# Order of small steps at three joins of a one-core encoder layer on Trainium2: weight parts of the down product, operands of the second branch, a weight cast, and the early weight parts

## The chip, the cores and the metric

The kernel runs on one core of one Trainium2 chip. The metric is the device time of one execution in microseconds (us). The kernel before has a median of 1955.72 us over 3 runs (1953.15 to 1956.71).

The engines are named as the profile names them: PE is TensorE (matmul), PEld its weight load, DVE is VectorE, ACT is ScalarE, POOL is GpSimd, SP is SyncE. SP and POOL issue most of the DMAs; each engine works through its own queue in order.

## The reference, cut to what matters

One layer, for a prompt of 1024 frames and a sample of 32 frames (1056 columns in the kernel, kept as four groups of 264), model width 1024, all in float32:

```python
h = rms_norm(x);  z = h @ w_in                       # q, k, v, gates ...
ya = sink_attention(...);  yb = hgrn2(...)
mix = sigmoid(ga) * (ya @ w_br_a) + sigmoid(gb) * (yb @ w_br_b)
x = x + rms_norm(mix @ w_out, g_post_mix)
a, u = split(rms_norm(x) @ w_up, 2)                  # D_FF = 2816 each
a = conv3(a) + b_conv
x = x + rms_norm((gelu(a) * u) @ w_down, g_post_ffn)
x = x + (pe @ w_ple) * sigmoid(x @ w_ple_gate)
```

The change touches three places of it: the two branch products (`w_br_a`, `w_br_b`) with the mix, the product with `w_out`, and the passage from the last piece of `w_up` to the product with `w_down`.

## The kernel before, in words

**Precision.** Every float32 operand is split into a high and a low part (fp32r). A product is three matmuls: high by high, high by low, low by high. So each weight tile needs, ahead of its product, a load, an ACT cast (the high part) and a DVE subtraction (the low part). In the input and output projections this is `load_next` (L177: ACT L184 and DVE L186). In a variant of it, chosen by `lo_by`, the low part is made by ACT (L188, the negated weight) and a POOL DMA that adds the weight to it (L189). In the branch products it is L228 (ACT) and L229 (DVE). In the up product it is L2029 and L2030, in the down product L2136 and L2137.

**Fewer products.** The branch, up and down products use a seven-product scheme for 2 by 2 blocks: of each unit, seven weight combinations ("parts", index i from 0 to 6) meet seven operand combinations, and DVE and ACT combine the seven results. A part of the branch product is 24 matmuls of 264 columns (two column pieces p, four k slices, three products each).

**Stages around the change.**

- *Branch stage* (849 to about 1020 us of the span). The operands of branch 0 are in tiles `oa`, those of branch 1 in tiles `ob`. For branch 1, `a_load` (L1554) loads an `ob` tile from memory on SP's queue, `b_rest` (L1558) loads more on POOL's, and `a_split` casts it (ACT L1561) and subtracts (DVE L1562, 128 x 1056). `during(s, f, ...)` puts a step into the program behind product number s of the stage; `beside` runs it there. The weights of this stage come in tiles `wa` (SP, L1530). ACT also copies results out of the PSUM banks here (`as`, L1671), and DVE combines them (L1689, L1691, L1693).
- *Out projection* (from 1019.8 us). Its first two weights, called w0 and w1 here, are loaded (`raw_next`) and cast (`load_next` with `lo_by` "dma") while the last branch products run. Blocks of 24 matmuls follow (L205 to L207); between them stand the transposes of `p` (L1980, results copied by DVE L229 into `pc`), the squares of the norm (L1830) and the **early parts**: `early_parts` makes the first seven parts of the up weight and the two halves of `w_ple` in three buffers (`pw`, `place`) and stores each to memory (`pw_d`, POOL, L2066, L2073, L2075). A buffer is written again only when its store has landed. One `next(early)` stands behind each of the nine blocks of `E_AT`.
- *Up units* (to about 1615 us), 22 of them with seven products each. `prepare(n)` makes the part that is AHEAD (3) products later. In the last unit the operands of the down product (`dop`) are loaded and split, too.
- *Down product*. `d_raw` loads two raw parts into one `wd` tile (two buffers, so the fourth load waits until the second tile has been read by L2136 and L2137). `d_prepare(n)` casts parts up to number n and loads two tiles ahead. Its first products go to fresh PSUM banks (three of them), and `evacuate` copies them out by ACT (L2513) to `S_`, `T1_` and the accumulators `acc`. The page that holds `S_` is the one that DVE reads last in the up unit (`Sp`: L2402, L2406, L2409).

**What sets the order.** The kernel is written with a tile framework whose scheduler may move instructions of an engine ahead of one another where no dependency forbids it. `with behind(S, V):` pins the instructions of its block behind what ACT (`S`) and DVE (`V`) were given so far; `behind()` without an engine pins nothing. So both the place in the program and the pin decide where an instruction stands in its engine's queue.

Of the kernel before, what the change touches and what calls it, by code (L numbers as in the profile page):

```python
# [10 lines left out]
F32 = mybir.dt.float32  # L11
# [6 lines left out]
P = 128  # L18
# [3 lines left out]
NF = 22  # L22
# [3 lines left out]
T = 1056  # L26
# [4 lines left out]
H = 264  # L31
# [28 lines left out]
def layer_kernel(  # L60
# [1523 lines left out]
    with right("mp") as mp:  # L1584
# [132 lines left out]
        def during(s, f, *a):  # L1717
            steps_a.setdefault(s, []).append((f, a))
# [14 lines left out]
        for n, (i, p) in enumerate(((2, 1), (3, 0), (3, 1))):  # L1733
            during(2 * n + 1, both, a_split, i, p)
        for n, (i, p) in enumerate((i, p) for i in range(3) for p in range(2)):
            during(18 + 2 * n, a_page, i, p, 1)
            during(18 + 2 * n, a_load, i, p, dma, 1)
            during(19 + 2 * n, b_rest, i, p)
            during(23 + 2 * n, both, a_split, i, p, 1)
        for n, (i, p) in enumerate((i, p) for i in (3, 4, 5) for p in range(2)):  # L1740
            during(34 + n + n // 2, a_page, i, p, 1)
            during(34 + n + n // 2, a_load, i, p, dma, 1)
            during(35 + n + n // 2, b_rest, i, p)
            during(38 + n + n // 2, both, a_split, i, p, 1)
        for p in range(2):
            during(44 + p, a_page, 6, p, 1)
            during(44 + p, a_load, 6, p, dma, 1)
# [5 lines left out]
        for n in range(2):  # L1753
            during(32 + n, mix_load)
            during(54 + 2 * n, raw_next)
            during(57 + 2 * n, both, load_next)
        n_s = [0]

        def beside(n):
# [332 lines left out]

    def prepare(n):

        if n >= 7 * NF:
            d_prepare(n - 7 * NF)
        while n_parts[0] < min(n + 1, 7 * NF):
            u, i = divmod(n_parts[0], 7)
            if i == 0:
                if u not in raw_w:  # L2100
                    unit_raw(u)
                s1 = wp.tile([P, 4, P], F32, tag="wb", name=nm("sa"), bufs=8)[:]
                gens[u] = unit_parts(u, s1, part_tile, lambda i, t: ready_w.append(t))
# [40 lines left out]
    for p in range(2):  # L2144
        for c in range(8):
            if p == 0 and c == 1:
                lo_by[0] = "vector"
            if p and c == 5:
                load_ple()
            with behind(*((S, V) if (p, c) == (0, 1) else ())):  # L2150
                w = next_w(2 + (p and c > 3) - (p + c == 0))
            for g in (2 * p, 2 * p + 1):
                z_out(c, g, block(w, ALL, Ra[g], Rb[g], KO if g % 2 else KS, H))
                if p == 0 and 2 * c + g in E_AT:
                    with behind(*((S, V) if c == 0 else ())):
# [199 lines left out]
    def up_unit(u):  # L2355
# [62 lines left out]
                 (3, Y, False, (3, 8)), (4, Z, False, (4, 6)), (5, Y, False, (2, 5)))  # L2418
        for ps, steps in (((0,), first_), ((1,), early)) if u == 0 else (((0, 1), order),):
            for n, (i, t, first, then) in enumerate(steps):  # L2420
                if u:
                    prepare(7 * u + n + AHEAD)
                elif ps == (1,):
                    with behind(S, V):
                        prepare(n + AHEAD + 2)
                mults(i, t, first, ps)
                if u == NF - 1:
                    if n == 0:
                        d_raw()
                        d_raw()  # L2430
                    if i < 3:
                        for p in range(2):
                            load_op(0, p, i, gdma)
                    if n in (3, 5, 6):
                        split_ops(0, {3: 0, 5: 1, 6: 2}[n])
                if ps == (1,) and n == 1:
                    with behind(E):
                        x1_t.append(pair_norm(1, 1.0 / D, late=True))
                if ps == (1,) and n == 4:
                    with behind(E):  # L2440
                        x1_t[0]()
                for a in then:
                    with behind(*((V,) if ps == (0,) and a == 2 else ())):
                        after(a, ps)
                if n == 1:
                    with behind(V):
                        tail_rest(u)
                if u == 1 and n == 3:
                    with behind(V):
                        tail_rest(0)  # L2450
                if u > 1 and n == 2 + u % 2:
                    if u % 2 == 0:
                        sums_of.append(act_sums(u // 2 - 1))
# [9 lines left out]
    for u in range(NF):  # L2463
        if u == 1:
# [5 lines left out]

    ep = ctx.enter_context(right("ep"))
    nrm = ep.tile([P, 4, 8], F32, name="nrm")
    T1_ = ep.tile([P, 4, 2, H], F32, tag="T1", name="T1")
    acc_t = [ep.tile([P, 4, 2, H], F32, name=f"acc{i}") for i in range(3)]
    last_sums = act_sums(NF // 2 - 1, acc_t[0][:].rearrange("p a b c -> p (a b c)")[:, 0:T + 2],
                         gdma)
    acc_t = [acc_t[1], acc_t[2], acc_t[0]]
    S_ = page(lq, 3, [P, 4, 2, H], "S").bitcast(F32)

    def acc_of(c):  # L2480
# [62 lines left out]
    def d_unit(pt, ph, c, ps=(0, 1), ws=None, beside=None):  # L2543
# [4 lines left out]
        kept = []  # L2548
        for n, i in enumerate(OPS[ph]):
            if ws is None:  # L2550
                d_prepare(n_d[0] + D_AHEAD)
                w = ready_d[n_d[0]]
                n_d[0] += 1
            else:
                w = ws[n]
            kept.append(w)
            t, first = banks[i]
            d_mults(w, pt, i, t, first, ps)
            evacuate(pt, c, i, t, ps)
# [385 lines left out]
```

## Time and profile before

| | |
|---|---|
| median of 3 runs | 1955.72 us |
| profiled execution, time | 1960.47 us |
| its span | 1958.8 us, mean granted PE clock 0.995 |
| PE busy | 1925.3 us (98%) |
| DVE, ACT, POOL busy | 1476.1, 1029.2, 378.9 us |
| DMA, mean | 168 GB/s |

How to read it: times in the trace count from the span's start. In a row of the timeline, the bracket behind an instruction gives the idle time of its engine ahead of it, and what ended that. In a row of the windows stand the stretch, its length, the busy time of PE, PEld, DVE, ACT and POOL with the number of instructions, the granted PE clock, the DMA engines' share and GB/s. In a row of the waits stand an engine, operation and line, what ended its waits, their sum, their number and the longest. In the chain of waits the time is what each piece contributed, which can be less than the instruction's duration.

### The profile page before, as it was taken

What the parts mean: (1) busy time and instruction counts of PE and PEld (TensorE: products, weight loads), DVE (VectorE), ACT (ScalarE), POOL (GpSimd) and SP (SyncE); (2) the same over time, 40 slices, a digit from 0 to 9 for tenths busy, and PEclk for the clock granted to TensorE, in tenths of its full rate; (3) what the DMA queues carried; (4) which work ended last, traced back from release to release, by engine and by line L of the source; (5) the groups of instructions that cost most, each with busy time, mean ns of one, the idle gap of its engine ahead of it and who ended that gap; (6) DMA issues with size and microseconds to landing.
All of it is one profiled execution on the core that took longest, in us unless ns stands there. A gap on an engine that the chain in (4) does not pass through costs nothing.

```text
span 1958.8 us, 38169 instructions
## 1 busy us (share of the span) xinstructions
PE 1925.3 (98%) x14523; PEld 1906.3 (97%) x14523; DVE 1476.1 (75%) x3201; ACT 1029.2 (53%) x2214; POOL 378.9 (19%) x530
## 2 busy tenths in 40 slices
PE   8999999999999999999999999999999998999999
PEld 8999999999999999999999999999999998999998
DVE  6777777788888888666785778788787876668872
ACT  7667777666656666553435763333333336534432
POOL 2111211001101001123221113444645330000000
PEclk9999999999999999999998999999999999999999
DMA  8544543455547354599978584566897456655443
GB/s 266 151 113 122 135 124 98 136 114 138 144 115 181 108 123 87 160 300 286 284 217 278 185 280 128 162 174 189 152 195 172 125 190 195 211 181 159 120 133 89
DMA packets 319599, 329.11 MB, mean 168 GB/s; under 512 B 17432, under 2 KB 277435, under 8 KB 319416
## 3 DMA queue, kind: packets, MB, share of 16 engines
q1 hardware_dynamic: 274152, 218.92, 36.2%
q0 software_dynamic: 45136, 107.70, 23.1%
q8 instruction: 114, 1.87, 0.4%
q14 instruction: 69, 0.57, 0.1%
q10 hardware_dynamic: 128, 0.06, 0.0%
HBM read 234.48 MB, written 132.47 MB: 187 GB/s over the span
## 4 chain that ended last, share of the span: by engine, by line
PE 83%; DVE 5%; DMA 4%; issue 4%; ACT 3%; POOL 0%; SPq 0%; ACTq 0%; DVEq 0%; POOLq 0%
PE st L2374 7%; PE st L2373 7%; PE st L2372 7%; PE st L2498 4%; PE mm L205 4%; PE st L2500 4%; PE mm L207 4%; PE st L2499 4%; PE mm L206 4%; PE st L205 2%; PE st L206 2%; PE st L207 2%; PE Y L1122 2%; PE Y L1125 2%; PE Y L1124 2%
## 5 line engine op out<-in xcount | busy, mean ns | idle before, releaser
L2372 PE MATMUL st<-op,wt 128*128 128x264 f32 x1232 | 348.7, 283 | 1.6 <-DMA wt<-pw_d 0.5
L2374 PE MATMUL st<-op,wt 128*128 128x264 f32 x1232 | 349.8, 284 | 0.0
L2373 PE MATMUL st<-op,wt 128*128 128x264 f32 x1232 | 347.7, 282 | 0.0
L2372 PEld LDWEIGHTS st<-op,wt 128*128 128x128 f32 x1232 | 231.2, 188 | 3.2 <-ACT Sp L2384 0.9
L2373 PEld LDWEIGHTS st<-op,wt 128*128 128x128 f32 x1232 | 231.4, 188 | 0.0
L2374 PEld LDWEIGHTS st<-op,wt 128*128 128x128 f32 x1232 | 230.8, 187 | 0.0
L2498 PE MATMUL st<-dop,wt 128*128 128x264 f32 x616 | 175.4, 285 | 6.3 <-ACT S L2513 6.3
L2500 PE MATMUL st<-dop,wt 128*128 128x264 f32 x616 | 175.3, 285 | 0.0
L2499 PE MATMUL st<-dop,wt 128*128 128x264 f32 x616 | 174.9, 284 | 0.0
L2029 ACT CAST wt<-wu 128x512 fp32r<-128x512 f32 x126 | 76.1, 618 | 177.3 <-POOL wu L2038 69.9
L205 PE MATMUL mm<-La,wh 128*128 128x384 f32 (+1 forms) x480 | 158.2, 330 | 0.0
L206 PE MATMUL mm<-Lb,wh 128*128 128x384 f32 (+1 forms) x480 | 155.3, 324 | 0.6 <-DVE Lb L784 0.4
L207 PE MATMUL mm<-La,wl 128*128 128x384 f32 (+1 forms) x480 | 154.9, 323 | 0.1
L2498 PEld LDWEIGHTS st<-dop,wt 128*128 128x128 f32 x616 | 116.7, 190 | 6.8 <-ACT S L2513 6.7
L2030 DVE TENSOR_TENSOR wt<-wu,wt 128x512 fp32r<-128x512 f32 x126 | 86.4, 694 | 43.0 <-ACT wt L2029 43.0
L2499 PEld LDWEIGHTS st<-dop,wt 128*128 128x128 f32 x616 | 116.7, 189 | 0.0
L2500 PEld LDWEIGHTS st<-dop,wt 128*128 128x128 f32 x616 | 116.4, 189 | 0.0
L2136 ACT CAST wt<-wd 128x512 fp32r<-128x512 f32 (+1 forms) x84 | 49.0, 586 | 96.3 <-PE st L2500 73.5
L206 PEld LDWEIGHTS mm<-Lb,wh 128*128 128x128 f32 x480 | 90.4, 189 | 1.7 <-DVE Lb L784 1.4
L207 PEld LDWEIGHTS mm<-La,wl 128*128 128x128 f32 x480 | 90.2, 188 | 0.5 <-DVE wl L759 0.5
L1122 PE MATMUL G<-La,wt 128*128 128x288 f32 x288 | 90.4, 314 | 0.0
L205 PEld LDWEIGHTS mm<-La,wh 128*128 128x128 f32 x480 | 90.2, 188 | 0.2
(628 smaller groups left out, 6334.1 us busy)
## 6 DMA issues: line engine op xcount, KB each, us to landing
wu<-in_w_up_dram SPq DMA_DIRECT2D x42, 512.0 KB
wu<-in_w_in_dram SPq DMA_DIRECT2D x36, 512.0 KB
w_d<-in_w_down_dram POOLq DMA_DIRECT2D x24, 704.0 KB, 8.7
a_d<-Up SPq DMA_DIRECT2D x21, 528.0 KB
wr<-in_w_in_dram SPq DMA_DIRECT2D x21, 512.0 KB
s_d<-sm SPq DMA_DIRECT2D x40, 264.0 KB
dop<-s_d SPq DMA_DIRECT2D x16, 528.0 KB
wr<-in_w_out_dram SPq DMA_DIRECT2D x16, 512.0 KB
```

Source lines behind the costliest of these rows:

```text
L205: E.matmul(ps, wh, a, start=first and n == 0, stop=False)
L206: E.matmul(ps, wh, b, start=False, stop=False)
L207: E.matmul(ps, wl, a, start=False, stop=last and n == len(ks) - 1)
L1122: E.matmul(o, wh, x[0][k], start=first and k == 0, stop=False, skip_group_check=True)
L2029: S.copy(t[:, 0], src)
L2030: V.tensor_tensor(t[:, 1], src, t[:, 0].bitcast(F32), op=ALU.subtract)
L2372: E.matmul(o, wh, xh, start=first and k == 0, stop=False, skip_group_check=True)
L2373: E.matmul(o, wh, xl, start=False, stop=False, skip_group_check=True)
L2374: E.matmul(o, wl, xh, start=False, stop=k == 3, skip_group_check=True)
L2498: E.matmul(o, wh, xh_, start=first and k == 0, stop=False, skip_group_check=True)
L2499: E.matmul(o, wh, xl_, start=False, stop=False, skip_group_check=True)
L2500: E.matmul(o, wl, xh_, start=False, stop=k == ng - 1, skip_group_check=True)
```

## The change

Four edits; nothing that is computed changes.

1. *Branch stage*. The steps of the second branch's operands get other numbers: loads of the first six at 20 + 2n - n//5 (before 18 + 2n), their splits at 28 + n (before 23 + 2n); the next six loads 2 later, their splits at 41, 42, 44, 45, 46, 47 (before 38, 39, 41, 42, 44, 45).
2. *Second out weight*. The step that casts w1 stands at 58, before at 59.
3. *Early parts*. Each `next(early)` is pinned behind ACT and DVE; before, only the first (c = 0) was.
4. *Last up unit and start of the down product*. The two first `d_raw` stand ahead of the unit's first `prepare`; from the unit's second product on, one down part is made for each product, six in all (before: one for each of its last three, inside `prepare`, when the number passed the end of the up parts, and three more ahead of the first down product). The down parts made at the first two units of the down product are pinned behind ACT and DVE. `T1_` and the three accumulators change places in memory with each other.

```diff
@@ branch stage
-            during(18 + 2 * n, a_page, i, p, 1)
-            during(18 + 2 * n, a_load, i, p, dma, 1)
-            during(19 + 2 * n, b_rest, i, p)
-            during(23 + 2 * n, both, a_split, i, p, 1)
+            m = 20 + 2 * n - n // 5
+            during(m, a_page, i, p, 1)
+            during(m, a_load, i, p, dma, 1)
+            during(m + 1, b_rest, i, p)
+            during(28 + n, both, a_split, i, p, 1)
...
-            during(38 + n + n // 2, both, a_split, i, p, 1)
+            during((41, 42, 44, 45, 46, 47)[n], both, a_split, i, p, 1)
...
-            during(57 + 2 * n, both, load_next)
+            during(57 + n, both, load_next)
@@ prepare
-        if n >= 7 * NF:
-            d_prepare(n - 7 * NF)
@@ out projection
-                    with behind(*((S, V) if c == 0 else ())):
+                    with behind(S, V):
                         next(early)
@@ up_unit
+                if u == NF - 1 and n == 0:
+                    d_raw()
+                    d_raw()
                 if u:
-                    prepare(7 * u + n + AHEAD)
+                    prepare(min(7 * u + n + AHEAD, 7 * NF - 1))
+                    if u == NF - 1 and n:
+                        d_prepare(n - 1)
...
-                    if n == 0:
-                        d_raw()
-                        d_raw()
@@ memory of the down product
+    acc_t = [ep.tile([P, 4, 2, H], F32, name=f"acc{i}") for i in range(2)]
     T1_ = ep.tile([P, 4, 2, H], F32, tag="T1", name="T1")
-    acc_t = [ep.tile([P, 4, 2, H], F32, name=f"acc{i}") for i in range(3)]
+    acc_t.insert(0, ep.tile([P, 4, 2, H], F32, name="acc2"))
@@ d_unit
-                d_prepare(n_d[0] + D_AHEAD)
+                with behind(*((S, V) if pt + ph == 0 and c < 2 else ())):
+                    d_prepare(n_d[0] + D_AHEAD)
```

The line numbers of the changed kernel are one higher than before from edit 1 to `prepare`, one lower from there to the end of the up product, and one higher in the down product.

**Where the instructions stand now.** First ACT at the passage from the up product to the down product, before (S is the first result of the down product, copied out; wt from wd are casts of down parts, dop casts of the down product's operands):

```order
L2136 CAST wt_19923<-wd_19687 128x384
L2345 CAST dop_19759<-dop_19759 128x792
L2136 CAST wt_19929<-wd_19860 128x384
L2345 CAST dop_19761<-dop_19761 128x792
L2136 CAST wt_19932<-wd_19860 128x384
L2136 CAST wt_19959<-wd_19926 128x384
L2136 CAST wt_19987<-wd_19926 128x384
L2513 COPY S_19920<-st_19921 128x528
```

And of the change:

```order
L2135 CAST wt_19843<-wd_19773 128x384
L2344 CAST dop_19725<-dop_19725 128x792
L2344 CAST dop_19727<-dop_19727 128x792
L2135 CAST wt_19875<-wd_19773 128x384
L2344 CAST dop_19765<-dop_19765 128x792
L2344 CAST dop_19767<-dop_19767 128x792
L2514 COPY S_19932<-st_19933 128x528
L2258 ACTIVATE a_19910<-ab_19655,cvec 128x1058
L2135 CAST wt_19959<-wd_19840 128x384
```

The two casts of the fourth raw tile (wd_19926 before, wd_19840 now) stood ahead of the first copy S and stand behind it. The same place on DVE, before (Sp is the page that S takes over):

```order
L2395 TENSOR_TENSOR Up_15042<-st_19653,Sp_14756 128x2x264
L2137 TENSOR_TENSOR wt_19929<-wd_19860,wt_19929 128x384
L2265 TENSOR_TENSOR Up_15042<-Up_15042,rbT 128x1056
L2137 TENSOR_TENSOR wt_19932<-wd_19860,wt_19932 128x384
L2402 TENSOR_TENSOR Sp_14756<-Sp_14756,st_19654 128x528
L2137 TENSOR_TENSOR wt_19959<-wd_19926,wt_19959 128x384
L2406 TENSOR_TENSOR ab_19655<-Sp_14756,rbT 128x2x232
L2409 TENSOR_TENSOR ab_19655<-Sp_14756,rbT 128x32 x2
```

And of the change:

```order
L2394 TENSOR_TENSOR Up_15042<-st_19653,Sp_14756 128x2x264
L2345 TENSOR_TENSOR dop_19765<-dop_19765 128x792
L2345 TENSOR_TENSOR dop_19767<-dop_19767 128x792
L2264 TENSOR_TENSOR Up_15042<-Up_15042,rbT 128x1056
L2401 TENSOR_TENSOR Sp_14756<-Sp_14756,st_19654 128x528
L2405 TENSOR_TENSOR ab_19655<-Sp_14756,rbT 128x2x232
L2408 TENSOR_TENSOR ab_19655<-Sp_14756,rbT 128x32 x2
```

No subtraction of a down part stands between the last readers of Sp any more; two subtractions of dop tiles stand there instead of two of parts.

Second, DVE in the out projection at the second half of w_ple, before (pw_13227 and pw_13226 are buffers of the early parts, pc the transposed p, wl the low part of an out weight):

```order
L229 TENSOR_TENSOR pc_13386<-tr_13424,pc_13386 128x264
L2074 TENSOR_TENSOR pw_13227<-rs_13225,pw_13226 128x1024
L186 TENSOR_TENSOR wl_13549<-wr_13546,wh_13548 128x1024
L1830 TENSOR_TENSOR sqz_13155<-sqz_13155,sq_13459 128x264
L2074 TENSOR_TENSOR pw_13226<-rs_13225,pw_13226 128x1024
L1830 TENSOR_TENSOR sqz_13154<-sqz_13154,sq_13497 128x264
L229 TENSOR_TENSOR pc_13504<-tr_13500,pc_13504 128x264
L186 TENSOR_TENSOR wl_13623<-wr_13620,wh_13622 128x1024
```

And of the change:

```order
L186 TENSOR_TENSOR wl_13782<-wr_13779,wh_13781 128x1024
L1831 TENSOR_TENSOR sqz_13155<-sqz_13155,sq_13687 128x264
L2075 TENSOR_TENSOR pw_13227<-rs_13225,pw_13226 128x1024
L1831 TENSOR_TENSOR sqz_13154<-sqz_13154,sq_13730 128x264
L229 TENSOR_TENSOR pc_13737<-tr_13733,pc_13737 128x264
L186 TENSOR_TENSOR wl_13890<-wr_13887,wh_13889 128x1024
L1831 TENSOR_TENSOR sqz_13155<-sqz_13155,sq_13766 128x264
L2075 TENSOR_TENSOR pw_13226<-rs_13225,pw_13226 128x1024
L229 TENSOR_TENSOR pc_13737<-tr_13773,pc_13737 128x264
```

The two subtractions L2074 (L2075 now) both moved back by four out weights (L186), and stand one behind each block of E_AT instead of close together.

Third, ACT at the end of the branch stage, before (wr_12881 is w0, wr_12956 is w1; Ra is made from the mixed branches ta):

```order
L184 CAST wh_12994<-wr_12881 128x1024
L188 ACTIVATE wl_12995<-wr_12881 128x1024
L228 CAST Ra_12164<-ta_12802 128x264
L228 CAST Ra_12166<-ta_12802 128x264
L228 CAST Ra_12567<-ta_12844 128x264
L228 CAST Ra_12569<-ta_12844 128x264
L228 CAST Ra_12567<-ta_12919 128x264
L228 CAST Ra_12569<-ta_12919 128x264
L184 CAST wh_13069<-wr_12956 128x1024
L188 ACTIVATE wl_13070<-wr_12956 128x1024
```

And of the change:

```order
L184 CAST wh_12994<-wr_12881 128x1024
L188 ACTIVATE wl_12995<-wr_12881 128x1024
L228 CAST Ra_12159<-ta_12802 128x264
L228 CAST Ra_12161<-ta_12802 128x264
L184 CAST wh_13032<-wr_12956 128x1024
L188 ACTIVATE wl_13033<-wr_12956 128x1024
L228 CAST Ra_12565<-ta_12844 128x264
L228 CAST Ra_12567<-ta_12844 128x264
L228 CAST Ra_12565<-ta_12919 128x264
L228 CAST Ra_12567<-ta_12919 128x264
```

The two instructions for w1 stand ahead of four casts that wait for DVE's mixing.

In the branch stage the queue of SP keeps its order: the loads L1554 of the `ob` tiles stand between the same loads L1530 of `wa` tiles as before. On ACT the casts L1561 of the `ob` tiles stand two to four weight casts later, and on DVE the subtractions L1562 with them; the copy `as` that stood behind two of these casts at 952 us stands ahead of them.

More of the change, by code (lines that the diff above doesn't have):

```diff
@@ L1735, in layer_kernel @@
         for n, (i, p) in enumerate((i, p) for i in range(3) for p in range(2)):
-            during(18 + 2 * n, a_page, i, p, 1)
-            during(18 + 2 * n, a_load, i, p, dma, 1)
-            during(19 + 2 * n, b_rest, i, p)
-            during(23 + 2 * n, both, a_split, i, p, 1)
+            m = 20 + 2 * n - n // 5
[3 more added lines that the diff above has]
+            during(28 + n, both, a_split, i, p, 1)
         for n, (i, p) in enumerate((i, p) for i in (3, 4, 5) for p in range(2)):
-            during(34 + n + n // 2, a_page, i, p, 1)
-            during(34 + n + n // 2, a_load, i, p, dma, 1)
-            during(35 + n + n // 2, b_rest, i, p)
-            during(38 + n + n // 2, both, a_split, i, p, 1)
+            during(36 + n + n // 2, a_page, i, p, 1)
+            during(36 + n + n // 2, a_load, i, p, dma, 1)
+            during(37 + n + n // 2, b_rest, i, p)
+            during((41, 42, 44, 45, 46, 47)[n], both, a_split, i, p, 1)
         for p in range(2):
@@ L2472, in layer_kernel @@
     nrm = ep.tile([P, 4, 8], F32, name="nrm")
+    acc_t = [ep.tile([P, 4, 2, H], F32, name=f"acc{i}") for i in range(2)]
     T1_ = ep.tile([P, 4, 2, H], F32, tag="T1", name="T1")
-    acc_t = [ep.tile([P, 4, 2, H], F32, name=f"acc{i}") for i in range(3)]
-    last_sums = act_sums(NF // 2 - 1, acc_t[0][:].rearrange("p a b c -> p (a b c)")[:, 0:T + 2],
+    acc_t.insert(0, ep.tile([P, 4, 2, H], F32, name="acc2"))
+    last_sums = act_sums(NF // 2 - 1, acc_t[2][:].rearrange("p a b c -> p (a b c)")[:, 0:T + 2],
                          gdma)
-    acc_t = [acc_t[1], acc_t[2], acc_t[0]]
     S_ = page(lq, 3, [P, 4, 2, H], "S").bitcast(F32)
```

## The prediction

> **What bounds the kernel now.** The page comes first: PE against the span.
>
> ```profile
> span 1958.8 us, 38169 instructions
> ...
> PE 1925.3 (98%) x14523; PEld 1906.3 (97%) x14523; DVE 1476.1 (75%) x3201; ACT 1029.2 (53%) x2214; POOL 378.9 (19%) x530
> ```
>
> PE is idle for 1958.8 - 1925.3 = 33.5 us in all. The change alters no matmul, so it can win these 33.5 us and whatever PE loses by running slower than it could; nothing else. Next, the waits of PE, longest sums first (sum, number, longest):
>
> ```profile
> PE st L2498 <- ACT S L2513: 6.3, 2, 5.6
> PE tr L1980 <- DVE pc L229: 2.9, 1, 2.9
> PE st L1663 <- ACT wt L228: 2.7, 1, 2.7
> ```
>
> Single waits make up these sums, so I looked for their places in PE's timeline:
>
> ```profile
> 910.19 0.36 PE L1663 MATMUL st<-oa,wt 128*128 128x264 f32 x1 [2.74 <-ACT wt L228]
> ...
> 952.58 0.39 PE L1663 MATMUL st<-ob,wt 128*128 128x264 f32 x1 [1.47 <-ACT as L1671]
> ...
> 1028.83 0.59 PE L207 MATMUL mm<-Ra,wl 128*128 128x264 f32 x1 [2.66 <-DMA wl<-wr]
> ...
> 1063.27 0.70 PE L1980 MATMUL tr<-ident,pr 88*128 88x88 f32 x3 [2.92 <-DVE pc L229]
> ...
> 1620.86 0.59 PE L2498 MATMUL st<-dop,wt 128*128 128x264 f32 x1 [5.57 <-ACT S L2513]
> ```
>
> The first two lie in the branch stage (edit 1), the third is the product that waits for w1 (edit 2), the fourth stands behind the early parts (edit 3), the fifth opens the down product (edit 4). Together 15.4 of the 33.5 us. The windows add what follows a gap; the last three numbers are the granted PE clock, the DMA share and GB/s:
>
> ```profile
> 910.00:913.00 3.00, 2.81 (x23) 2.84 (x24) 2.81 (x5) 1.70 (x3) 1.16 (x2) 1.00 0.24 70
> ...
> 1029.00:1032.00 3.00, 3.00 (x15) 3.00 (x16) 0.69 (x1) 1.88 (x6) 0.23 (x1) 0.55 0.60 179
> 1032.00:1042.00 10.00, 10.00 (x85) 10.00 (x84) 6.29 (x9) 5.35 (x11) 1.78 (x4) 1.00 1.05 311
> ...
> 1052.00:1063.00 11.00, 8.35 (x70) 8.14 (x68) 4.49 (x6) 6.97 (x14) 1.77 (x4) 0.97 0.98 315
> 1063.00:1066.00 3.00, 2.73 (x13) 2.73 (x14) 2.38 (x5) 1.07 (x2) 1.12 (x2) 0.50 0.77 241
> 1066.00:1070.00 4.00, 4.00 (x24) 4.00 (x23) 1.91 (x3) 1.84 (x6) 0.12 (x1) 0.59 0.91 230
> ...
> 1620.00:1623.00 3.00, 2.14 (x9) 2.15 (x10) 1.92 (x7) 2.58 (x4) 0.00 (x0) 0.50 0.39 110
> 1623.00:1626.00 3.00, 3.00 (x16) 3.00 (x16) 2.67 (x4) 0.78 (x2) 0.00 (x0) 0.56 0.30 78
> ```
>
> Undisturbed, PE runs 85 matmuls in 10.00 us, 0.118 us each: a block of 24 is 2.8 us, a down product of 18 is 2.1 us. After three of the gaps it runs at about half the clock. The loss is busy time x (1 - clock): 3.00 x 0.45 = 1.35 us after the gap at 1028; 2.73 x 0.50 + 4.00 x 0.41 = 3.0 us after 1063; 2.14 x 0.50 + 3.00 x 0.44 = 2.4 us after 1620; none after 910. So the gaps are worth: w1 2.66 + 1.35 = 4.0, early parts 2.92 + 3.0 = 5.9, down start 5.57 + 2.4 = 8.0.
>
> The Trainium skill, TensorE: Matmul & The Clock Gate, section What's actually happening, ties the half rate to at least one idle window of about 3.4 us. By that rule the gaps of 2.66 and 2.92 us would cost no clock and the sum below would be 4.3 us smaller; the trace speaks against it, since both are followed by a clock of 0.5 to 0.6. It also says that the window runs freely; that fits 2.74 us at 910 passing unpunished.
>
> **Edit 4, the down start.** The chain of waits into the 5.57 us gap, and two rows of DVE ahead of it:
>
> ```profile
> 1610.32 7.82 DMA wd<-in_w_down_dram
> ...
> 1618.78 0.56 DVE wt L2137
> 1619.34 0.55 DVE ab L2406
> ...
> 1620.20 0.61 ACT S L2513
> ```
>
> ```profile
> 1607.91 1.87 DVE L2346 TENSOR_TENSOR dop<-dop 128x792 fp32r<-128x792 f32 x2
> ...
> 1612.89 0.69 DVE L2402 TENSOR_TENSOR Sp<-Sp,st 128x528 f32<-128x528 f32 x1
> 1618.78 0.56 DVE L2137 TENSOR_TENSOR wt<-wd,wt 128x384 fp32r<-128x384 f32 x1 [5.19 <-ACT wt L2136]
> ```
>
> The fourth raw tile's load takes 7.82 us; DVE's L2137 for it stands ahead of L2406, the last reader of the page that S takes, and so the copy S and PE wait for a part that is needed only six products later. The order of the change has L2402, L2406, L2409 with no L2137 between, and on ACT the copy S with no cast of that tile ahead. S then follows L2402: that ended at 1613.58; from the end of the L2137 to the copy's start L2406, L2409 and the hand-over took 1620.20 - 1619.34 = 0.86, the copy 0.61: 1615.05. Two subtractions of dop (0.93 each) stand ahead in place of two of parts (0.55 each): + 0.8, 1615.85. PE stopped at 1620.86 - 5.57 = 1615.29. About 0.6 us of gap is left; I charge it no clock, since 2.74 us at 910 cost none. The second unit's copies, and T and acc behind them on ACT, get 0.4 us more. Gain 8.0 - 1.0 = 7.0; the bounds are 8.0 and, if the dop subtractions wait for their loads, 3.5 (half the gap back with its clock). What is next late is the fourth tile itself, part 6: its load waits for L2137 of part 3, which the order now has ahead of the dop pair that ran at 1607.91, so it starts at about 1607 and with 7.82 us lands at 1615; PE needs it six products of 2.1 us after 1615.3, at 1628. That cover is gone only if the load takes about 20 us.
>
> **Edit 3, early parts.**
>
> ```profile
> 1061.30 1.23 DVE L2074 TENSOR_TENSOR pw<-rs,pw 128x1024 fp32r<-128x1024 f32 x1 [4.15 <-DMA pw_d<-pw]
> ...
> 1062.79 0.43 DVE L229 TENSOR_TENSOR pc<-tr,pc 128x264 fp32r<-128x264 f32 x1
> ```
>
> ```profile
> 1053.24 7.97 DMA pw_d<-pw
> ```
>
> L2074 writes a buffer whose store was issued at 1053.24 and landed 7.97 us later; the copy `pc` that frees PE's next transpose waits behind it. Pinned, the two L2074 stand four out weights later, one per two blocks (5.7 us). The second of them needs the buffer stored behind the first half: a store of 7.97 us in a spacing of 5.7 us leaves DVE blocked for about 2 us, with the last `pc` behind it; no transpose of p follows that copy, so I charge 0.5 us; at worst the 2 us stop PE with half as much again in clock, 3.0. POOL's stores come one per two blocks as well and keep its loads of x behind them; these feed nothing before the norm. Gain 5.4, bounds 2.9 and 5.9.
>
> **Edit 2, w1.**
>
> ```profile
> 1016.55 0.73 ACT L228 CAST Ra<-ta 128x264 fp32r<-128x264 f32 x2 [5.08 <-DVE ta L1693]
> ...
> 1018.13 1.05 ACT L188 ACTIVATE wl<-wr 128x1024 fp32r<-128x1024 f32 x1
> ```
>
> ```profile
> 1011.00 0.55 POOL L1633 DMA_DIRECT2D ma<-mx_d  x1 [1.44 <-DVE ta L1693]
> 1019.48 0.87 POOL L189 DMA_DIRECT2D wl<-wr  x1 [7.93 <-ACT wl L188]
> ...
> DMA to landing us min/median/max: 5.1/7.2/9.3
> ```
>
> The adding DMA L189 issues at 1019.48, takes 9.3 us and lands at 1028.8: the gap. L184 and L188 now stand ahead of the four Ra casts that wait for DVE's mixing. ACT sat idle from 1016.55 - 5.08 = 1011.47 for the last of these; two casts of 1.05 us fit into that, so L188 ends by about 1013.6 and POOL, which has issued L1633 at 1011.00 and waits for nothing else, issues L189. With the 9.3 us it lands at 1022.9; PE wants it at 1028.83 - 2.66 = 1026.2. The Ra casts behind are hidden in the same idle time. Gain 4.0; bounds 4.0 and, if the transfer takes over 12.6 us, 0.
>
> **Edit 1, the branch stage.**
>
> ```profile
> 895.06 12.93 DMA wa<-wa_d
> ```
>
> ```profile
> 908.74 0.69 DVE L229 TENSOR_TENSOR wt<-wa,wt 128x512 fp32r<-128x512 f32 x1 [6.35 <-ACT wt L228]
> ...
> 911.46 1.25 DVE L1562 TENSOR_TENSOR ob<-ob 128x1056 fp32r<-128x1056 f32 x1
> ```
>
> ```profile
> 950.96 1.07 ACT L1561 CAST ob<-ob 128x1056 fp32r<-128x1056 f32 x1
> 951.94 0.59 ACT L1671 COPY as<-st 128x528 f32<-128x528 f32 x1
> ```
>
> ```profile
> 976.00:1000.00 24.00, 23.98 (x197) 23.77 (x197) 23.34 (x40) 9.37 (x21) 6.39 (x11) 1.00 0.66 194
> ```
>
> The gap at 910 comes from a wa load of 12.93 us beside the ob loads; L229 for it and, behind that, L1689, which frees PE's bank, wait. SP's order of these loads does not change, and L229 stays ahead of L1689, so this gap stays: 0 gained. At 952 the copy `as` stood behind a cast of ob (0.98 to its start) that the change puts behind it: gain 1.0. Against that, subtractions L1562 move later, two of them (1.25 us each) into a stretch where DVE is busy 23.34 of 24.00 us; I charge 0.5, bounds 0 and 2.5. Net gain 0.5.
>
> **Sum.** 7.0 + 5.4 + 4.0 + 0.5 = 16.9 us, against the profiled execution 1960.47 (span 1958.8), giving 1943.6. That execution is 4.75 above the median of the runs; taking the same difference from 1955.72 gives 1938.8.
>
> **The rivals.**
>
> *The out projection is bound by its transfers.* The DMA share is 1.05 and 0.98 in its windows. If so, the 9.4 us won by edits 2 and 3 come back as waits for out weights: 16.9 - 9.4 = 7.5 gained, 1948.2. Against: no wait for an out weight's load is among PE's long ones, and the share falls to 0.91 and 0.77 later. The Trainium skill, DMA: Bandwidth & Descriptors, section Issuing engines are not separate DMA queues, says that all issuers' transfers share the same 16 engines; that is the case for this rival.
>
> *Half the gap at the down start comes back*, through the dop subtractions: 7.0 becomes 2.5 to 3.5, about 4 less, 1942.8 to 1943.3.
>
> Both together: 16.9 - 9.4 - 4.0 = 3.5, 1952.2, no change.
>
> *The loads do get out of each other's way at 895*, because their waits end at other times: 2.74 more, 1936.1. For: the steps are numbered later. Against: SP's order is the same.
>
> *Slower: pinned early parts block ACT and DVE.* Each part from the fourth on writes a buffer stored about four blocks (11.3 us) earlier; pinned, nothing behind it on DVE or ACT (out weights' casts, `pc`) can pass. The point is a store of over 11.3 us. Six such parts at 14 us would stop PE 6 x 2.7 us, and about half as much again in clock: 24.3 us, with edit 3's gain gone as well: 24.3 - 11.5 = 12.8 slower, 1968.5. For: 12.93 us has been seen for a transfer. Against: these stores took 7.97.
>
> **How the numbers follow.** A measurement of this kernel can tell about 0.2%, 3.9 us, from no change. Forecast 0.58, ob loads clear 0.06, half the down gap back 0.12, transfers bind 0.10: faster 0.86. Both together and the like: same 0.09. Slower 0.05. The range reaches from the case with the loads clear and no residue, 1934, to the transfer-bound one with its own uncertain 3 us, 1951.
>
> **What would show it.** In the profile of the changed kernel: no PE wait above 1.5 us at L207, L1980 or at the first down product; clock 1.00 through 1026 to 1070 and at 1615 to 1626 (all some us earlier); S about 1.5 us behind L2402's end; L189's second issue before 1014 on the clock of before; the gap near 910 still there. I am wrong if new waits on out weights appear, if DVE waits on pw_d stores several times, or if S still follows a L2137.

## The result and the profile after

In runs taken side by side the changed kernel has a median of 1944.17 us (1941.47 to 1947.66, 6 runs), the kernel before 1957.97 (1953.15 to 1960.84, 6 runs): ratio 0.9933, 95% interval 0.9915 to 0.9951. That is 13.1 us less (9.6 to 16.6). The prediction was 1938.8 us, 16.9 less, in a range of 1934 to 1951: right direction, inside the range, the gain somewhat too large. The profiled execution of the change took 1947.46 us.

The page of the change, span and PE:

```profile
span 1945.8 us, 38169 instructions
...
PE 1921.6 (99%) x14523; PEld 1903.9 (98%) x14523; DVE 1472.6 (76%) x3201; ACT 1028.7 (53%) x2214; POOL 381.4 (20%) x530
```

PE's idle time is now 1945.8 - 1921.6 = 24.2 us, before 33.5. PE's own busy time is 3.7 us smaller with the same matmuls: less of it ran at the slow clock. PE's waits in the change:

```profile
PE st L1663 <- DVE ac L1689: 3.1, 2, 2.7
PE st L2499 <- ACT S L2514: 2.6, 2, 1.9
PE tr L747 <- POOL ident masks.py:199: 2.5, 1, 2.5
PE st L1663 <- ACT as L1671: 2.1, 3, 1.2
PE mm L656 <- DMA x<-in_x_prompt_dram: 1.7, 1, 1.7
```

The waits at L207 and L1980 are gone, and of the 6.3 us at the first down products 2.6 are left. The third and the last line belong to the kernel's start, where nothing was changed. The two longest gaps that are left inside the changed stages:

```profile
912.23 0.36 PE L1663 MATMUL st<-oa,wt 128*128 128x264 f32 x1 [2.66 <-DVE ac L1689]
...
1622.53 0.39 PE L2499 MATMUL st<-dop,wt 128*128 128x264 f32 x1 [1.90 <-ACT S L2514]
```

And the windows of the change around these, where the gaps of w1 and of the early parts were, and at the kernel's start:

```profile
9.00:12.00 3.00, 2.27 (x12) 1.90 (x11) 2.10 (x7) 1.59 (x4) 1.71 (x5) 0.50 1.09 358
...
912.00:915.00 3.00, 2.77 (x17) 2.80 (x18) 2.80 (x6) 0.88 (x2) 1.10 (x2) 0.75 0.25 66
...
1029.00:1032.00 3.00, 3.00 (x27) 3.00 (x26) 2.29 (x4) 1.74 (x4) 0.56 (x1) 1.00 1.03 258
1060.00:1063.00 3.00, 3.00 (x28) 3.00 (x27) 2.50 (x5) 2.11 (x7) 0.84 (x2) 1.00 1.05 370
...
1623.00:1626.00 3.00, 3.00 (x18) 3.00 (x17) 2.73 (x5) 2.41 (x5) 0.00 (x0) 0.58 0.41 131
```

In the out projection PE is full at clock 1.00, at a DMA share of 1.03 and 1.05. The gap near 910 is still there and is followed by a slow clock this time; a new gap of 1.90 us stands at the third copy S, with a clock of 0.58 behind it.

**Stage by stage.** Where in the kernel the time went shows in the distance between fixed instructions of PE: the first branch product (L1663), the first out block (L205), the transposes of the norm (L308), the first down product (L2498, later L2499), and the gate product that waits for ACT's wg. The starts of these rows give, in us, for all profiled executions of this study (the experiments follow below):

| | branch | out | up | down |
|---|---|---|---|---|
| before | 169.8 | 69.6 | 521.2 | 238.8 |
| the change | 172.0 | 59.2 | 520.5 | 234.5 |
| the change, second execution | 170.0 | 59.2 | 520.8 | 233.5 |
| edit 1 alone | 169.4 | 67.1 | 521.4 | 238.9 |
| edit 2 alone | 168.2 | 66.8 | 521.0 | 237.8 |
| edit 3 alone | 168.4 | 63.7 | 521.2 | 238.4 |
| edit 4 alone | 169.2 | 68.7 | 520.6 | 232.9 |
| without edit 1 | 169.5 | 59.5 | 520.4 | 232.2 |
| part 7 with part 6 | 169.9 | 59.2 | 520.7 | 232.0 |
| ob loads pinned | 168.8 | 59.2 | 520.4 | 232.9 |
| both additions | 174.0 | 59.2 | 521.0 | 232.2 |
| without the pin of edit 4 | 169.2 | 59.2 | 520.7 | 238.0 |
| without one part per product | 170.2 | 59.2 | 521.5 | 235.9 |
| without new places | 171.9 | 59.2 | 520.7 | 233.4 |

Between the two first rows: branch +2.2, out -10.4, up -0.8, down -4.4.

### The profile page after: what moved, and what is told of

Its sections match the earlier page's. It is cut to its first block, busy times and chain, and to the rows that moved or that the text cites. A ratio compares the mean times of both kernels' runs of the same rounds, so it can differ in the third digit from the quotient of the medians.

```text
span 1945.8 us, 38169 instructions
## 1 busy us (share of the span) xinstructions
PE 1921.6 (99%) x14523; PEld 1903.9 (98%) x14523; DVE 1472.6 (76%) x3201; ACT 1028.7 (53%) x2214; POOL 381.4 (20%) x530
## 4 chain that ended last, share of the span: by engine, by line
PE 85%; DVE 6%; DMA 3%; ACT 3%; issue 2%; POOL 0%; SPq 0%; ACTq 0%; DVEq 0%; POOLq 0%
PE st L2373 7%; PE st L2372 7%; PE st L2371 7%; PE mm L205 4%; PE mm L206 4%; PE mm L207 4%; PE st L2499 4%; PE st L2501 4%; PE st L2500 4%; PE st L1663 2%; PE st L1665 2%; PE st L1667 2%; PE st L205 2%; PE st L206 2%; PE st L207 2%
## 5 line engine op out<-in xcount | busy, mean ns | idle before, releaser
L2499 PE MATMUL st<-dop,wt 128*128 128x264 f32 x616 | 175.2, 285 | 2.6 <-ACT S L2514 2.6
L205 PE MATMUL mm<-La,wh 128*128 128x384 f32 (+1 forms) x480 | 158.3, 330 | 0.0
L207 PE MATMUL mm<-La,wl 128*128 128x384 f32 (+1 forms) x480 | 155.0, 323 | 0.1
L2499 PEld LDWEIGHTS st<-dop,wt 128*128 128x128 f32 x616 | 116.3, 189 | 3.1 <-ACT S L2514 3.0
L207 PEld LDWEIGHTS mm<-La,wl 128*128 128x128 f32 x480 | 90.3, 188 | 0.5 <-DVE wl L759 0.5
L205 PEld LDWEIGHTS mm<-La,wh 128*128 128x128 f32 x480 | 90.4, 188 | 0.0
```

Source lines behind the costliest of these rows:

```text
L205: E.matmul(ps, wh, a, start=first and n == 0, stop=False)
L207: E.matmul(ps, wl, a, start=False, stop=last and n == len(ks) - 1)
L2499: E.matmul(o, wh, xh_, start=first and k == 0, stop=False, skip_group_check=True)
```

## The experiments

A kernel's time varies by up to 5 us around its median between executions (the kernel before, 31 runs: 1950.94 to 1960.62), so the intervals of the ratios below are some 2 to 3 us wide on each side, and the stages decide more than the totals.

**Each edit alone.** Four kernels, each the kernel before with one of the four edits of the diff and nothing else. Edit 1 alone (the `during` numbers of the ob loads and splits):

> The kernel before with edit 1 alone. Theory: edit 1 takes away the gap of 1.47 us near 952 and nothing else; the gap near 910 (2.74 us before, 2.66 in the change) stays, since the order of the loads is the same; what the branch stage lost in the change's profile (171.97 us from its first product to the first out block, before 169.76) is spread between executions and not the edit. Expected: stage about 168.3 to 170, time 0 to 1.5 us below before. Rival: the later casts and subtractions cost, stage about 172, time 2 us above before.

Measured: ratio 1.0006 (0.9993 to 1.0018), branch stage 169.4 us. The gap near 950 did not go:

```profile
950.47 0.39 PE L1663 MATMUL st<-ob,wt 128*128 128x264 f32 x1 [1.03 <-ACT as L1671]
```

and the one near 910, which the edit was to leave alone, was absent in this execution. So both gaps are less fixed than theory and prediction had them. What the edit does cost, in another place, is shown under "Spread and edit 1".

Edit 2 alone:

```diff
-            during(57 + 2 * n, both, load_next)
+            during(57 + n, both, load_next)
```

> The kernel before with edit 2 alone. Theory: the gap of 2.66 us ahead of the first L207 product and its slow clock go, 4.0 us; from the first out block to the transposes of the norm (69.6 us before) about 65.6; the gap behind the early parts stays. Rival: the stage is bound by its transfers, so the 4 us come back as a longer gap behind the early parts or as waits for out weights, stage 69 us.

Measured: ratio 1.0006 (0.9996 to 1.0017), out projection 66.8 us (before 69.6; 67.1 and 68.7 in the executions of edits 1 and 4 alone). The gap at w1 is gone. The one behind the early parts at L1980, which was expected to stay, is absent in this execution, and this one stands a few blocks later, in PE's timeline:

```profile
1032.63 0.39 PE L205 MATMUL mm<-Ra,wh 128*128 128x264 f32 x1 [3.02 <-ACT wh L184]
1034.27 0.59 PE L207 MATMUL mm<-Ra,wl 128*128 128x264 f32 x1 [1.14 <-DVE wl L186]
```

ACT's timeline says why:

```profile
1029.19 0.62 ACT L2029 CAST pw<-rw 128x512 fp32r<-128x512 f32 x1 [4.23 <-DMA pw_d<-pw]
...
1031.50 2.02 ACT L184 CAST wh<-wr 128x1024 fp32r<-128x1024 f32 x2
```

An early part's cast, moved forward by the scheduler, waits 4.23 us for the store of its buffer, and the casts L184 of the next out weights stand behind it. So the rival was right that the time comes back, and wrong about the cause: it is a place in ACT's queue that edit 3 clears.

Edit 3 alone:

```diff
-                    with behind(*((S, V) if c == 0 else ())):
+                    with behind(S, V):
```

> The kernel before with edit 3 alone. Theory: the gap of 2.92 us at the transpose of p and the slow clock behind it go, 5.9 us; from the first out block to the transposes of the norm 63.7 us instead of 69.6; the gap at w1 stays at about 2.7 us. Rival (transfers bind): under 3 us gained.

Measured: ratio 0.998 (0.9967 to 0.9993), out projection 63.7 us as expected (though that was counted from the 69.6 us of one execution), no gap at L1980, and the one at w1 still there:

```profile
1027.27 0.39 PE L207 MATMUL mm<-Ra,wl 128*128 128x264 f32 x1 [2.35 <-DMA wl<-wr]
```

The four combinations of edits 2 and 3 are then: neither 68.5 (mean of before, edit 1 and edit 4 alone), edit 2 alone 66.8, edit 3 alone 63.7, both 59.2. Together they win 9.3 us, alone 1.7 and 4.8: each is worth 2.8 us more beside the other.

Edit 4 alone:

> The kernel before with edit 4 alone. Theory: as in the whole change, the gap of 5.57 us at the first down product goes, and one of about 1.9 us with a slow clock behind it comes at the third copy S, since the sixth raw tile's load waits for the subtraction of part 7, which stands behind the last unit's tail on DVE; from the first down product to the first gate product 230.8 us instead of 235.2, 4.4 us gained. Rival: that later gap is a matter of that execution or of the other edits; then 7 us gained, 228 us.

Measured: ratio 0.9988 (0.9976 to 1.0), down stage 232.9 us against 237.8 to 238.9 in the four profiles without edit 4, 4.9 to 6.0 less (the expectation counted to the first gate product; the table counts to the one that waits). The later gap is there without the other edits, with a granted clock of 1.00 behind it:

```profile
1629.44 0.39 PE L2498 MATMUL st<-dop,wt 128*128 128x264 f32 x1 [1.82 <-ACT S L2513]
```

**Spread and edit 1.** The changed kernel a second time, and the change without edit 1.

> The changed kernel once more, unaltered, for a second profiled execution and more times. Theory: the gaps of the branch stage differ between executions by a few us (168.2 to 169.8 us in four profiles of the old order, 169.4 and 172.0 in two of the new), so this one's stage lies between 169 and 172, and the gap of about 1.9 us at the third copy S, which has a fixed cause, is there again. Rival: edit 1 costs 2 us every time, stage 172 again. Time 1944 either way.

Measured: median 1943.5, ratio 0.994 (0.9928 to 0.9952), branch stage 170.0. The gap near 910 was 0.56 us this time. The gap at the third copy S is there again, longer, but with no slow clock behind it:

```profile
1619.85 0.39 PE L2499 MATMUL st<-dop,wt 128*128 128x264 f32 x1 [2.20 <-ACT S L2514]
```

```profile
1620.00:1623.00 3.00, 3.00 (x26) 3.00 (x27) 2.42 (x4) 2.59 (x5) 0.00 (x0) 1.00 0.42 131
```

> The change without edit 1. Theory (spread, not the edit): time within 1.5 us of the changed kernel's 1944, branch stage 168 to 170 us, the gap of 1.5 us near 950 back in some executions. Rival (edit 1 costs 2 us): time 1942, stage 168.5.

Measured: median 1943.02, ratio 0.994 (0.9926 to 0.9954), branch stage 169.5, no gap near 950 and one of 0.51 us near 910. Over all executions the branch stage took 168.2 to 169.8 us with the old numbers (five) and 169.2 to 172.0 with the new (seven); the means are 169.0 and 170.4. Where this difference arises shows when PE's matmuls of the stage are counted from its first one. The two groups are level up to about 905 us, before anything that edit 1 moves. Near 910, where the gap comes and goes, they part by 0.35 us. The rest, about 1.0 us, arises in one stretch, the 192 matmuls that run from 973.05 to 996.69 in the profile before. They take 23.5 to 23.7 us in all five profiles with the old numbers, and 24.3 to 25.6 us in all nine with the new ones (the two with pinned loads, below, included). Before, and in the change, the window of this stretch (its x195 counts a few more matmuls of PE than the 192) and the ob subtractions that DVE does in it:

```profile
973.05:996.69 23.64, 23.62 (x195) 23.41 (x194) 22.28 (x37) 9.96 (x20) 5.42 (x9) 1.00 0.61 182
L1562 DVE TENSOR_TENSOR ob<-ob x3: 1250/1252/1252, 975.7 to 985.5; 128x1056 fp32r<-128x1056 f32 x3
```

```profile
974.92:999.23 24.31, 24.14 (x195) 23.57 (x193) 23.11 (x36) 9.40 (x20) 5.20 (x9) 1.00 0.56 165
L1562 DVE TENSOR_TENSOR ob<-ob x5: 1252/1252/1253, 977.0 to 989.5; 128x1056 fp32r<-128x1056 f32 x5
```

Three subtractions in each of the five old profiles, five in each of the nine new ones, while DVE is busy almost throughout. PE's part of it is split into waits too short to stand out in a list of gaps; the only one that the change's timeline names here is 0.16 us at 993.29, behind DVE's L1689. So edit 1 costs about 1 us on the mean (0.7 to 2.0 in the nine profiles), and that it wins something is not seen. Its rival was right in kind, with half the size.

**The gap at the third copy S.** The kernel is the change with

```diff
-                with behind(*((S, V) if pt + ph == 0 and c < 2 else ())):
-                    d_prepare(n_d[0] + D_AHEAD)
+                with behind(*((S,) if pt + ph == 0 and c < 2 else ())):
+                    d_prepare(n_d[0] + D_AHEAD + (n_d[0] == 1))
```

The theory comes from the changed kernel's trace. ACT, up to the copy S that PE waits for at 1622.53:

```profile
1619.39 0.52 ACT L2135 CAST wt<-wd 128x384 fp32r<-128x384 f32 x1 [3.28 <-DMA wd<-w_d]
1619.81 0.59 ACT L2514 COPY acc<-st 128x528 f32<-128x528 f32 x1
1620.31 0.85 ACT L2344 CAST dop<-dop 128x792 fp32r<-128x792 f32 x1
1621.06 0.93 ACT L2135 CAST wt<-wd 128x384 fp32r<-128x384 f32 x2
1621.88 0.60 ACT L2514 COPY S<-st 128x528 f32<-128x528 f32 x1
```

The cast at 1619.39 waits for the sixth raw tile. SP issued that load late:

```profile
1614.62 0.34 SPq L2124 DMA_DIRECT2D wd<-w_d  x1
```

since its buffer is read last by the subtraction of part 7 on DVE (the second row L2136 here), which stands behind the last unit's tail (L2266 to L2272):

```profile
1611.09 1.23 DVE L2271 TENSOR_TENSOR Up<-a,Up 128x1024 f32<-128x1024 f32 x1 [1.16 <-ACT a L2267]
...
1612.34 0.55 DVE L2136 TENSOR_TENSOR wt<-wd,wt 128x384 fp32r<-128x384 f32 x1
...
1614.04 1.03 DVE L2136 TENSOR_TENSOR wt<-wd,wt 128x384 fp32r<-128x384 f32 x2
```

> The change, with down part 7 made together with part 6 one product earlier, and these parts pinned behind ACT alone, so that their subtractions may stand ahead of the last unit's tail on DVE. Theory: the sixth raw tile's load is then issued some 4 us earlier, lands by 1615, and the gap of 1.9 us at the third copy S goes with its slow clock: from the first down product to the first gate product 227.5 us instead of 230.8, time 3 us below the changed kernel. Rival: the load is slow for another reason, or the next tile takes its place: still 230 us.

Measured: the load is issued 3.9 us earlier, counted from each profile's first down product (1602.13 in the change, 1600.68 here); the gap at the third copy S is gone, and a smaller one stands at the fourth. SP, and PE:

```profile
1609.23 0.34 SPq L2124 DMA_DIRECT2D wd<-w_d  x1
```

```profile
1626.65 0.39 PE L2499 MATMUL st<-dop,wt 128*128 128x264 f32 x1 [0.73 <-ACT S L2514]
```

The gap is also gone in the version with both additions (below), and it is there, 1.2 to 2.2 us long, in all seven other profiles that have the pin of edit 4: its cause is shown. What it is worth is not. The down stage is 232.0 us here, 234.5 and 233.5 in the two executions of the change, but also 232.2 without edit 1, where the gap was 1.19 us. The median is 1944.22, ratio 0.994 (0.9928 to 0.9952), no difference from the change that a measurement can tell. The 3 us expected were too many, since the slow clock behind this gap came in one of the seven profiles only, the change's first.

**The gap near 910.**

```diff
-            during(m, a_load, i, p, dma, 1)
+            during(m, pinned, a_load, i, p, dma, 1)
```

where `pinned` runs its step in `with behind(nc.sync)`, behind what SP was given so far.

> The change, with the loads of the first six ob tiles pinned on SP's queue where edit 1 numbers them, so that they really come later, one between each pair of wa loads. Theory: the wa load that took 12.9 us shared the DMA engines with these six loads; the gap of 2.7 us near 910 goes, branch stage 166.5 to 168 us, time 2 to 3 us below the changed kernel. Rival: the other transfers (ta, mx, wa itself) fill the engines, and the gap stays or another opens at the first ob product, stage 170 us or more.

Measured: ratio 0.9938 (0.9921 to 0.9955), median 1941.77, branch stage 168.8, above the 166.5 to 168 expected. Nothing near 910, a small gap at 927:

```profile
927.82 0.36 PE L1663 MATMUL st<-oa,wt 128*128 128x264 f32 x1 [0.34 <-DVE ac L1678]
```

One execution with a short stage settles nothing here: the gap near 910 was also absent with the loads in their old order (edit 1 alone, edit 3 alone). With both additions together:

> The change with both additions that removed a gap in their own profiles: ob loads pinned on SP, and part 7 made with part 6, pinned behind ACT alone. Theory: branch stage 168 to 169 us, from the first down product to ACT's wg wait of the gate product 232 us (233.5 and 234.5 in two profiles of the change), no gap at the third copy S; time 1 to 2.5 us below the changed kernel, 1941 to 1943. Rival: what one addition wins moves to another wait, time as the change.

Measured: median 1943.56, ratio 0.9927 (0.9913 to 0.9941). The down stage is 232.2 and the gap at the third S gone, as expected; the branch stage took 174.0 us, with 3.9 us of gaps ahead of anything that was moved, and this one behind the pinned loads:

```profile
933.64 0.36 PE L1663 MATMUL st<-oa,wt 128*128 128x264 f32 x1 [1.28 <-DVE ac L1678]
```

Here the rival holds: a gap between 920 and 940 us stands in both profiles with pinned loads and in none of the other twelve. No version beats the change by more than the runs can tell.

**The parts of edit 4.** Without the pin (`d_prepare` as before, one part per product and the places kept):

> The change without the pin of edit 4 (behind ACT and DVE for the first two down units). On ACT three casts of later parts then stand ahead of the first copy S, the last of them of the fifth raw tile. Theory: the pin is what took the first gap away; without it the copy S waits until that tile has landed, about 1608 on the clock of the change's profile instead of 1605.5: a gap of about 3 us ahead of the third product's successor, with a slow clock; but part 7 is then made earlier and the gap at the third copy S goes. Down start to the gate's wait 233 to 236 us. Rival: the earlier raw loads alone took the gap away, so none of 3 us comes back.

Measured: ratio 0.9957 (0.994 to 0.9974), down stage 238.0 us, all of edit 4's gain lost. PE, and ACT ahead of the copy:

```profile
1608.34 0.59 PE L2499 MATMUL st<-dop,wt 128*128 128x264 f32 x1 [5.12 <-ACT S L2514]
```

```profile
1606.68 1.11 ACT L2135 CAST wt<-wd 128x384 fp32r<-128x384 f32 x2 [2.62 <-DMA wd<-w_d]
1607.70 0.59 ACT L2514 COPY S<-st 128x528 f32<-128x528 f32 x1
```

The mechanism is the expected one, and the third copy S has no gap; the first is 5.1 us long, not 3: its casts waited for their load until 1606.68, and since the down stage began 3.4 us earlier here, that is 1610.1 on the clock of the change's profile, not 1608. So the earlier loads alone win nothing, and the rival falls.

Without one part per product (the pin and the places kept):

> The change without edit 4's one part per product in the last up unit and its earlier raw loads (memory places and pin kept). Parts 3 to 5 are then made behind the first copy S and behind the last unit's tail on DVE. Theory: the pin without the earlier parts only moves the wait: PE waits about 4 us for part 3 or its low half in the second down unit, down start to the gate's wait 236 to 239 us, no gain over before's 238.5. Rival: the pin alone is enough, 233 us.

Measured: ratio 0.9939 (0.9924 to 0.9954), down stage 235.9. PE waits for part 3, for its cast and then for its low half:

```profile
1609.55 0.39 PE L2499 MATMUL st<-dop,wt 128*128 128x264 f32 x1 [1.28 <-ACT wt L2137]
1610.98 0.59 PE L2501 MATMUL st<-dop,wt 128*128 128x264 f32 x1 [0.93 <-DVE wt L2138]
```

2.2 us of waits, and a mean clock of 0.69 from 1609.55 to 1615.00, which costs another 1.4: 3.6 us, near the 4 expected. The pin alone wins 2.6 us (238.5 to 235.9), the parts made earlier another 2.6 (to 233.3, the mean of the change's two executions, edit 4 alone and the change without edit 1), and these only beside the pin. Without the new places of T and the accumulators:

> The change without the new places of T and the accumulators in memory. Theory: the places only decide which old tile a copy has to wait for; the copies T and acc wait for a reader up to 1 us longer, and the down product's start is up to 1 us longer than in the change (233.5 and 234.5 us to the gate's wait). Rival: they carry part of the gain, 236 us.

Measured: 233.4 us, one profile and one time (1946.94). One gap of 0.50 us at a copy T is new; those at the second and third copy S (0.69 and 1.54 us) are there as in the change. The places carry none of the gain that can be seen.

## Why the prediction was right or wrong

- **Edits 2 and 3: size right, terms wrong.** Predicted 4.0 + 5.4 = 9.4, measured 9.3 (68.5 to 59.2). But the prediction took them as independent and named nothing that is next late behind w1. Edit 2 alone opens a gap of 3 us at the out weights behind an early part on ACT; edit 3 takes that away as well. The sum came out because both were made. Counted from the execution that it was read in (69.6), the gain is 10.4; that 9.4 meets 9.3 is partly luck. The 0.5 us charged for the second L2075 did not come; it ran without a wait for a store. DVE in the change:

```profile
1073.74 1.23 DVE L2075 TENSOR_TENSOR pw<-rs,pw 128x1024 fp32r<-128x1024 f32 x1
```

- **w1's path was as worked out.** POOL issued the second L189 early, and it landed faster than the 9.3 us of before; PE did not wait. POOL's timeline in the change, and the answer on line L189:

```profile
1014.99 0.87 POOL L189 DMA_DIRECT2D wl<-wr  x1 [0.50 <-ACT Ra L228]
```

```profile
DMA to landing us min/median/max: 5.4/6.1/6.7
```

- **Edit 4: the step that failed is "what is next late is the fourth tile".** Its load did have cover. The sixth was late, behind the tail's DVE steps, and ACT's cast of it held up the third copy S: 1.9 and 2.2 us in the change's two executions, 1.2 to 2.2 in all seven profiles, with a slow clock behind it in one of them. Predicted 7.0, measured 5.2 (238.5, the mean of four executions, to 233.3). The first copy S itself came as computed, 1.0 us behind the end of L2401, and PE did not wait for it. DVE and ACT in the change:

```profile
1603.77 0.70 DVE L2401 TENSOR_TENSOR Sp<-Sp,st 128x528 f32<-128x528 f32 x1
```

```profile
1605.45 0.60 ACT L2514 COPY S<-st 128x528 f32<-128x528 f32 x1 [6.92 <-DVE ab L2408]
```

- **Edit 1: a loss where half a microsecond of gain was counted.** The prediction took 1.0 us for the gap at 952 and charged 0.5 for two subtractions L1562 that move to where DVE is full. The move is as it said, three of them becoming five, but it costs about 1.0 us. The 1.0 us of gain does not show: the gaps near 910 and 950 are not fixed properties of the order. In the executions with the old numbers the first was between nothing and 2.74 us and the second between nothing and 1.47; with the new ones between nothing and 2.78, and nothing and 1.03. The prediction read one execution as if it were the rule. The DMA share in that part of the stage (885 to 960) was 0.94 before, 0.95 and 0.98 in the change's two executions; that this is why the gaps come and go is not shown.
- **The base was a long execution.** The one profiled before took 1960.47 us; the median of 31 runs of the same kernel beside the single edits is 1955.88. Its out projection, 69.6 us, was the longest of three. Of the gaps read in it, w1's 2.66 us was the longest of four (1.93 to 2.40 in the other profiles that have it); the ones at the early parts and at the down start lie among the others (2.01 to 3.73, and 4.73 to 5.58). So a gap read from this one execution was uncertain by about 1 us, and the forecast gave its terms no such spread.
- **The sum.** By the means of the stages, 5.2 (down) + 9.3 (out) + 0.6 (up) - 1.4 (branch) = 13.7 us, against 13.1 by the medians (9.6 to 16.6) and 16.9 predicted. What is missing are 1.8 us at the down start and 1.9 in the branch stage; the 0.6 in the up stage was not forecast.
- **Rivals.** That transfers bind the out projection is refuted: 59.2 us in eight of the nine profiles that have edits 2 and 3, 59.5 in the other, with a DMA share of 1.03 and 1.05 in the change's windows above and no wait of PE over 0.3 us for an out weight. That half the gap at the down start comes back happened to a smaller part, 1.8 us of the 7.0, at another copy and for another cause. (By its own terms, 2.5 to 3.5 left of 7.0, that rival gives 1942.3 to 1943.3; the prediction has 1942.8 as the lower end.) That pinned parts block ACT and DVE did not happen.
- **The clock.** The sum counted 6.7 us of slow clock behind three gaps. PE's busy time fell by 3.7 us, but the change's execution has slow stretches of its own: behind 912, behind 1622, and at the kernel's start (0.50 from 9 us).

The 0.6 us in the up stage (521.2 to 520.6) go at least in part with edit 4: the last up unit takes 20.3 to 20.5 us in all nine profiles that make one down part per product in it, and 20.6 to 21.0 in the five that do not, the change without one part per product among them. Which of its steps does it was not tried.

## What to carry to other kernels

When a step is taken out of an in-order queue, look for the next step in that queue that waits for a transfer, and for what stands behind it: here two of the gaps that were removed, w1's and the one at the down start, had a second one behind them, and two edits were worth more together than apart. A gap behind loads can be a draw, not a number (0.56 and 2.66 us near 910 in two executions of the change): take two or three profiles before a gap of one or two microseconds is put into a sum. Stages measured between fixed instructions show an edit of 2 us that the total, with its spread of up to 5 to either side, does not; counting matmuls inside a stage shows one of 1 us, even where no gap stands out.

## What the runs showed of the hardware

Between 1.9 and 2.8 us, the length of a gap alone does not tell whether a slow clock follows. It came behind gaps of 1.90 us (the change, clock 0.58, above), 1.96 (without one part per product, near 910) and 2.17 (part 7 with part 6, near 878), and did not come behind 2.20 (the change's second execution, 1.00, above) and 2.74 (before, near 910, 1.00). The windows behind the second and the third of these:

```profile
912.00:915.00 3.00, 3.00 (x19) 3.00 (x18) 1.39 (x3) 0.44 (x1) 2.45 (x4) 0.63 1.00 278
```

```profile
879.00:882.00 3.00, 3.00 (x17) 3.00 (x16) 2.43 (x4) 2.03 (x4) 0.00 (x0) 0.52 0.71 213
```

The same gap at the same place, the third copy S, had it in one execution and not in the next. Over all fourteen profiles, from 849 to 1660 us, a slow clock followed 15 of the 16 gaps of 2.3 us or more (the 2.74 us that the prediction went by is the exception), 5 of the 7 from 1.9 to 2.3, and of the 22 from 1.0 to 1.9 only one, of 1.28 us, which has a second wait of 0.93 us 1.4 us after it. Behind the change's 1.90 us the clock, in steps of 1 us from 1622.53, was 0.96, 0.50, 0.50, 0.50, 0.83 and 1.00, a loss of 1.7 us. The Trainium skill, TensorE: Matmul & The Clock Gate, section What's actually happening, ties the half rate to at least one idle window of about 3.4 us and says that the window runs freely. That the same gap can have the slow clock or not fits a window that runs freely; that it takes 3.4 us of idle time does not fit the clock of 0.58 behind 1.90 us.
